# A float32 transpose on one core: PSUM evacuation split by halves, one copy for each evenly spaced run of ranges

## The chip, the cores and the metric

One core of one Trainium2 chip. The metric is the device time of one execution, in microseconds (us), as the median of several runs.

In the profiles PE is TensorE, PEld its weight loads, DVE is VectorE and ACT ScalarE; PEq and ACTq are the instruction streams of PE and of ScalarE, and L117 is a line of the kernel. PSUM is the memory into which PE transposes here, SBUF the one between it and the 16 DMA engines, which move the bytes in and out. A transfer has landed when its completion is signalled.

## The reference

```python
x = np.random.randn(8192, 8192).astype(np.float32)
def reference(x):
    return np.transpose(x)
```

268 MB are read and 268 MB written; nothing is computed.

## The kernel before

The input is cut into 128 chunks of 128 rows by 4096 columns, loaded whole into one of three buffers. PE transposes a chunk in 32 blocks of 128x128 into PSUM. Four blocks form a range `q` (512 columns of the input, 0 to 7), and a range is copied from PSUM to SBUF into a register: a buffer that gathers the same range of eight consecutive chunks, so that the store can write rows of 4 KB. The windows of the eight ranges are staggered, so in steady state one window closes, and is stored, in each chunk. There are nine registers for eight open windows: a window that opens in a chunk takes the register whose store was issued two chunks before.

```python
S = 32; B = 4; W = 8; NR = S // B; NIN = 3; NREG = 9
pss = [nc.alloc_psum_tensor(f"ps{k}", [P, 2 * B * P], dt).ap() for k in range(NR // 2)]
...
def transposes(k):                          # PE, one chunk
    nc.tensor.sem_inc(s_ld[k], -16).wait_op(s_ld[k], 16, "sem-ge")
    for h in range(NR // 2):
        if h < 2:                           # both copies of this engine in the last chunk are done
            n = NR // 4
            nc.tensor.sem_inc(s_bank[h], -n).wait_op(s_bank[h], n, "sem-ge")
        for b in range(2 * B):
            ...                             # transpose into pss[h]
        tr.then_inc(s_pe, 1)
...
for t, (s, c) in enumerate(chunks):
    for h in range(NR // 2):                # pairs of ranges (0,1) (2,3) (4,5) (6,7)
        e = h % 2
        eng = (nc.scalar, nc.vector)[e]     # ScalarE, VectorE, ScalarE, VectorE
        ...                                 # open windows; wait for the register's store
        eng.wait_ge(s_pe, t * NR // 2 + h + 1)
        for u in runs:                      # one run of two ranges, or two of one
            ...
            cp = nc.scalar.copy(out=o, in_=i) if e == 0 else nc.vector.tensor_copy(out=o, in_=i)
            ...
        for k in closing:
            store(*k)                       # issued by ScalarE, which first waits for that copy
    if t + NIN < T:
        nc.scalar.wait_ge(s_pe, (t + 1) * NR // 2)
        load(t + NIN)                       # issued by ScalarE too
```

ScalarE's stream therefore holds its copies, the waits for VectorE's copies whose windows close, and all stores and loads but the first three loads.

## Time and profile before

| | before |
|---|---|
| median of the first 3 runs | 1264.29 us (1264.04 to 1265.28) |
| PE busy | 742.7 us, 59% |
| VectorE busy | 316.1 us in 311 copies |
| ScalarE copies | 261.7 us in 320 copies |
| rate in mid-span, by fortieths of the span | 428 to 431 GB/s in most, 414 in the lowest |

Busy time is a share of the span, not of the critical path.

### The profile page before, as it was taken

The page shows a single profiled execution, that of the slowest core. Times are in us where ns is not written, and L with a number is a line of the kernel's source. Part 1 is how long each engine was busy: PE and PEld are TensorE (multiplying, and loading weights), DVE is VectorE, ACT ScalarE, POOL GpSimd, SP SyncE. Part 2 cuts the span into 40 slices and gives each one's busy share as a digit, 9 for nine tenths or more (in the row PEclk, how much of TensorE's full clock was granted, in tenths as well). Part 3 has the DMA queues.
Part 4 walks back from the last instruction along what each step waited for, and adds up shares of the span by engine and source line. Part 5 has one row for each costly group of instructions (what it writes and reads, how often), then busy time and mean ns, then how long its engine had stood idle before and what let it go on. Part 6 is the DMA issues. An engine that isn't in the chain of part 4 may idle for free. (4 is left out here: it accounts for less than half of the span.)

```text
span 1262.9 us, 9961 instructions
## 1 busy us (share of the span) xinstructions
PE 742.7 (59%) x4096; PEld 721.8 (57%) x4096; DVE 316.1 (25%) x311; ACT 263.0 (21%) x321; POOL 0.7 (0%) x6
## 2 busy tenths in 40 slices
PE   6565565665566555655566655666565655656561
PEld 5565555665566555655565655656565645655561
DVE  3322222222222222222222222222222222222220
ACT  3212121222122211212221121121212211122120
POOL 0000000000000000000000000000000000000000
PEclk9967768677777777686766687777868687777865
DMA  9999999999999999999999999999999999999998
GB/s 381 429 430 420 429 431 428 430 429 431 428 430 430 431 428 429 430 430 430 426 425 414 429 430 429 430 430 430 428 430 430 431 428 430 430 430 429 430 427 339
DMA packets 39274, 536.98 MB, mean 425 GB/s; under 512 B 4320, under 2 KB 4832, under 8 KB 6240
## 3 DMA queue, kind: packets, MB, share of 16 engines
q10 hardware_dynamic: 38832, 530.60, 98.8%
q1 hardware_dynamic: 432, 6.29, 1.2%
q14 instruction: 9, 0.07, 0.0%
q8 instruction: 1, 0.02, 0.0%
HBM read 268.44 MB, written 268.44 MB: 425 GB/s over the span
## 5 line engine op out<-in xcount | busy, mean ns | idle before, releaser
L117 PE MATMUL ps<-ident,in 128*128 128x128 f32 x4096 | 742.7, 364 | 493.1 <-PEq L114 493.1
L117 PEld LDWEIGHTS ps<-ident,in 128*128 128x128 f32 x4096 | 721.8, 219 | 513.9 <-issue 513.6
L208 DVE COPY regs<-ps 128x1024 f32<-128x1024 f32 (+1 forms) x311 | 316.1, 1034 | 921.2 <-PE ps L117 704.5
L208 ACT COPY regs<-ps 128x1024 f32<-128x1024 f32 (+1 forms) x320 | 261.7, 843 | 973.6 <-PE ps L117 654.9
L208 ACT ACT_TABLE_LOAD x1 | 1.3, 1283 | 0.9 <-SPq L69 0.9
L86 POOL TENSOR_SCALAR_AFFINE_SELECT ident<-ident 128x128 f32<-128x128 f32 x1 | 0.3, 293 | 0.2 <-POOL ident L84 0.2
L84 POOL MEMSET ident<- 128x128 f32 x1 | 0.2, 204 | 0.5 <-SPq L69 0.5
L241 POOL MEMSET const-bfloat16-1.0<- 128x1 bf16 x1 | 0.1, 102 | 0.0
L241 POOL MEMSET const-uint8-127<- 128x1 uint8 x1 | 0.1, 102 | 0.0
L241 POOL MEMSET const-float32-0.0<- 128x1 f32 x1 | 0.1, 99 | 0.2 <-issue 0.2
L241 POOL MEMSET const-float32-1.0<- 128x1 f32 x1 | 0.1, 99 | 0.0
## 6 DMA issues: line engine op xcount, KB each, us to landing
in<-in_x_dram ACTq DMA_DIRECT2D x125, 2048.0 KB, 22.5
out_dram<-regs ACTq DMA_DIRECT2D x114, 2048.0 KB, 18.4
out_dram<-regs ACTq DMA_DIRECT2D x4, 1792.0 KB, 17.5
in<-in_x_dram SPq DMA_DIRECT2D x3, 2048.0 KB, 11.6
out_dram<-regs ACTq DMA_DIRECT2D x4, 1536.0 KB, 15.1
out_dram<-regs ACTq DMA_DIRECT2D x4, 1280.0 KB, 16.7
out_dram<-regs ACTq DMA_DIRECT2D x4, 1024.0 KB, 16.6
out_dram<-regs ACTq DMA_DIRECT2D x4, 768.0 KB, 16.4
```

Of the source, the lines that this page charges most:

```text
L84: nc.gpsimd.memset(ident, 0.0).then_inc(s_id, 1)
L86: nc.gpsimd.affine_select(out=ident, in_=ident, compare_op=mybir.AluOpType.not_equal, fill=1.0, base=0, pattern=[[-1, P]], channel_multipl ...
L117: tr = nc.tensor.transpose(pss[h][:, b * P:(b + 1) * P], ins[k][:, j:j + B * P - B + 1:B], ident,)
L208: cp = nc.scalar.copy(out=o, in_=i) if e == 0 else nc.vector.tensor_copy(out=o, in_=i)
L241: nc = _bacc.Bacc("TRN2", target_bir_lowering=False, num_devices=1)
```

## The change

The intent: ScalarE takes ranges 0 to 3 and VectorE 4 to 7, each half in one PSUM tensor of four banks, so that up to four ranges whose places in the registers are evenly spaced go in one instruction. A half of PSUM is handed back to PE by one signal, after its last copy. A copy waits for the last range that it reads.

```diff
-        pss = [nc.alloc_psum_tensor(f"ps{k}", [P, 2 * B * P], dt).ap() for k in range(NR // 2)]
+        NH = NR // 2
+        pss = [nc.alloc_psum_tensor(f"ps{k}", [P, NH * B * P], dt).ap() for k in range(2)]
...
-            for h in range(NR // 2):
-                if h < 2:
-                    n = NR // 4
-                    nc.tensor.sem_inc(s_bank[h], -n).wait_op(s_bank[h], n, "sem-ge")
+            for q in range(NR):
+                e, g = divmod(q, NH)
+                if g == 0:
+                    nc.tensor.sem_inc(s_bank[e], -1).wait_op(s_bank[e], 1, "sem-ge")
...
-            for h in range(NR // 2):
-                e = h % 2
+            for e in range(2):
...
-                for q in (2 * h, 2 * h + 1):
+                for q in range(e * NH, (e + 1) * NH):
...
+                runs = []
+                for g in range(NH):
+                    if runs:
+                        ...          # same window length and the same gap as the run so far
+                            u.append(g)
+                            continue
+                    runs.append([g])
...
+                    eng.wait_ge(s_pe, t * NH + (e * NH + u[-1]) // 2 + 1)
...
-                for k in closing:
-                    store(*k)
+                    for q in ends:
+                        store(q, e, copied[e])
```

## The prediction

> **What bounds the kernel now.** I read the page's slices and its queue lines first, because a transpose computes nothing and must move every byte twice.
>
> ```profile
> DMA  9999999999999999999999999999999999999998
> GB/s 381 429 430 420 429 431 428 430 429 431 428 430 430 431 428 429 430 430 430 426 425 414 429 430 429 430 430 430 428 430 430 431 428 430 430 430 429 430 427 339
> ...
> q10 hardware_dynamic: 38832, 530.60, 98.8%
> q1 hardware_dynamic: 432, 6.29, 1.2%
> ...
> HBM read 268.44 MB, written 268.44 MB: 425 GB/s over the span
> ```
>
> The mean busy share of the 16 DMA engines is at least nine tenths in 39 of the 40 slices, and the two data queues' packets fill 98.8 + 1.2 = 100% of the 16 engines' time. The rate is flat at 428 to 431 GB/s between a ramp and a tail. No compute engine comes near: PE 59%, VectorE 25%, ScalarE 21% of 1262.9 us. The table of stretches says the same without the ends:
>
> ```profile
> 100.00:600.00 500.00, 298.56 (x1632) 290.33 (x1632) 125.62 (x120) 103.64 (x118) 0.00 (x0) 0.75 1.01 429
> 600.00:1100.00 500.00, 301.13 (x1632) 292.90 (x1632) 125.75 (x122) 104.03 (x123) 0.00 (x0) 0.74 1.01 428
> ```
>
> The last three columns are the granted clock, the DMA share and GB/s: share 1.01, so there is no hole between transfers to win back. At 429 GB/s a chunk's 2.097 MB in and 2.097 MB out take 4.89 us each, 9.78 us a chunk; 128 chunks make 1252 us, and what remains of the 1262.9 us span is the start (first transposes at 8.46 us) and the drain of the last stores.
>
> A bound DMA can still be starved if copies make issues late, so I then looked at one chunk's timeline (start us, length us, engine, what) and at how far ahead of need the transfers are issued:
>
> ```profile
> 444.96 6.14 PEld L117 LDWEIGHTS ps<-ident,in 128*128 128x128 f32 x32 [3.82 <-issue]
> 445.00 6.30 PE L117 MATMUL ps<-ident,in 128*128 128x128 f32 x32 [3.65 <-PEq L114]
> 446.99 1.01 ACT L208 COPY regs<-ps 128x1024 f32<-128x1024 f32 x1 [5.51 <-PE ps L117]
> 448.69 1.23 DVE L208 COPY regs<-ps 128x1024 f32<-128x1024 f32 x1 [6.09 <-PE ps L117]
> 450.39 1.01 ACT L208 COPY regs<-ps 128x1024 f32<-128x1024 f32 x1 [2.39 <-PE ps L117]
> 451.40 1.23 DVE L208 COPY regs<-ps 128x1024 f32<-128x1024 f32 x1 [1.48 <-PE ps L117]
> 452.66 0.55 ACTq L28 DMA_DIRECT2D out_dram<-regs  x1
> 453.24 1.23 ACTq L100 DMA_DIRECT2D in<-in_x_dram  x1
> ```
>
> ```profile
> in<-in_x_dram ACTq DMA_DIRECT2D x125, 2048.0 KB, 22.5
> out_dram<-regs ACTq DMA_DIRECT2D x114, 2048.0 KB, 18.4
> ```
>
> PE works 6.3 us of each 9.8 us and idles 3.65 us for the next load; each copy waits for PE. A load lands 22.5 us and a store 18.4 us after issue, though its own transfer takes 4.89 us. The very first load was issued at 0.94 us and its transposes began at 8.46 us: 7.5 us, so about 2.6 us of fixed latency above the 4.89. What is left is time spent behind other transfers: 22.5 - 4.9 - 2.6 = 15.0 us for a load, 18.4 - 4.9 - 2.6 = 10.9 us for a store. That is the slack: issues may come that much later before the DMA engines run dry.
>
> **What the Trainium skill says.** "DMA: Bandwidth & Descriptors", section Where 436 GB/s comes from, puts the ceiling of the 16 SBUF ports at 435.2 GB/s. The trace agrees: it sits at 428 to 431, 1 to 2% below. (The same section says that about 358 GB/s binds for HBM to SBUF; it also says that its single-core numbers are of one core with its neighbour idle, as one core runs here, and the trace shows 430.) "ScalarE: Activation LUTs", section What ACT_TABLE_LOAD costs, gives 186 ns + 0.833 ns per element for an ACTIVATE with immediate scale and bias, and an overlap of about 93 ns between back-to-back ones. The trace's two ScalarE forms, below, give 165 + 0.828 per element, and two adjacent 128x512 copies show 1.07 us together, not 2 x 589 ns. "VectorE: DVE Perf Modes", section Why PSUM operands drop a tier, says that an fp32 operand in PSUM holds VectorE at one element a cycle; the trace's 1.05 ns per element agrees with the page's 0.96 GHz. So VectorE is not sped up by a longer instruction.
>
> **The change part by part.** The rows by form:
>
> ```profile
> L208 DVE COPY regs<-ps 128x1024 f32<-128x1024 f32 x201 | 245.3, 1224 | 707.4 <-PE ps L117 542.0 <-DMA out_dram<-regs 163.9
> L208 ACT COPY regs<-ps 128x1024 f32<-128x1024 f32 x192 | 193.5, 1013 | 740.3 <-PE ps L117 486.9 <-DMA out_dram<-regs 209.9 <-DVE regs L208 39.9
> L208 DVE COPY regs<-ps 128x512 f32<-128x512 f32 x110 | 70.9, 686 | 213.8 <-PE ps L117 162.5 <-DMA out_dram<-regs 50.9
> L208 ACT COPY regs<-ps 128x512 f32<-128x512 f32 x128 | 68.7, 589 | 233.3 <-PE ps L117 168.0 <-DMA out_dram<-regs 50.4 <-DVE regs L208 7.2
> ```
>
> Each engine still copies 4 of 8 ranges of 512 elements per chunk, the same amount. What the built kernels' instruction streams show: ScalarE goes from 320 copies to 256 (40 of four ranges, 32 of three, 72 of two, 112 of one: 160 + 96 + 144 + 112 = 512 ranges), VectorE from 311 to 250 (45, 25, 77, 103). A longer copy, by the rows' slopes: ScalarE 424 ns per further range, so 589 + 3 x 424 = 1861 ns for four; VectorE 538 ns, so 686 + 3 x 538 = 2300 ns. Because neighbours overlap, a merged copy saves only 1.07 - 1.01 = 0.06 us on ScalarE and 1.29 - 1.23 = 0.06 us on VectorE (pairs of 128x512 in the timeline against one 128x1024). So ScalarE loses about 64 x 0.06 = 4 us of 262, VectorE 61 x 0.06 = 4 us of 316, all beside other work. The PE's transposes, and sizes, number and order of the transfers stay.
>
> What moves is when a range is copied. PE finishes a range every 6.3 / 8 = 0.79 us. Store issue after the start of PE's pass, before and after, no register wait, worst case of one copy of four:
> - ranges 0, 1: before one copy behind range 1, 2.0 + 1.0 + 0.1 = 3.1 us. After: behind range 3, 3.2 + 0.3 + 1.9 = 5.4. Later by 2.3.
> - ranges 2, 3: VectorE's first copy ended at 449.92, 5.0 us. After 5.4. Later by 0.4.
> - ranges 4, 5: ScalarE's second copy ended at 451.40, 6.4 us. After, on VectorE behind range 7: 6.3 + 0.2 + 2.3 = 8.8. Later by 2.4.
> - ranges 6, 7: 7.7 us (452.66 - 444.96). After 8.8. Later by 1.1.
>
> The load follows in ScalarE's stream: at worst at 8.8 + 0.6 = 9.4 us where it was 6.5 to 8.3, later by 3 us. All of this is set against slacks of 10.9 us (store) and 15.0 us (load), and the lateness does not add up from chunk to chunk as long as loads land every 9.8 us: the queue gets the same transfers in the same order, later by a constant. Sum on the path that sets the end: 0.
>
> PSUM: PE may start a half when that half's copies are done, ScalarE's at 5.4 us (6.6 if it first waits for a register, which the timeline shows freed 4.7 us after PE's start: 4.7 + 1.9), VectorE's at 8.8. The next pass begins at 9.8 and reaches the second half at 9.8 + 3.2. Neither waits.
>
> The ends. In the first chunks PE was held 0.29 to 0.46 us between passes by the last ScalarE copy; in the change that copy comes earlier, since ScalarE's ranges are PE's first four. The ramp loses about 1 us to a low rate (14 to 30 us: 400 GB/s in the mean against 430, 7% of 16 us), so at most some tenths can come back. At the end the eight closing stores have the same sizes and order and the same bytes to drain (2048 + 1792 + ... + 256 KB = 9.4 MB, 22 us at 430 GB/s). Sum: -0.3 us, so 1264.3 becomes 1264.0.
>
> **The rivals.**
> - *The stores' feedback becomes the bound.* There are 9 registers for 8 open windows, so a window opened at a chunk needs the store issued two chunks before; the waits view has 260 us of ScalarE and 215 us of VectorE waiting on stores, and now such a wait holds all four ranges of an engine. If the delays above were exposed, 0.2 us per chunk (25 / 128) would already be 2%, and 2 us per chunk would make 1500 us. Against it: the awaited store lands 4.7 us into PE's pass, before PE has finished the ranges, and the 10.9 us of slack is four times the delay.
> - *PE waits for PSUM.* Four banks are now released by one signal each, after one long copy. If PE slipped past the load it would show as a longer gap before its passes. It has 3.65 us of idle time per chunk, and VectorE's release at 8.8 us precedes the need at 13 us. Even if 1 us were exposed in each chunk, loads are 15 us ahead: 1264 still.
> - *It gets faster because ScalarE, which issues all but the first three transfers, is freer.* 4 us of 262 us is freed, but nothing moves faster. 536.98 MB at the skill's 435.2 GB/s is 1234 us without any ramp or drain; 2% faster is 1239, which leaves 5 us for a start and a tail that in steps of 2 us show 41 and 270 GB/s before full rate, and 208, 74 and 8 after it. Practically excluded.
>
> **Range and chances.** Three runs of before lie within 1.2 us. I add 2 us for a changed ramp or tail and for the phase of reads and writes against each other, either way: 1260.5 to 1267.5. Faster by over 2%: 0.01. Slower by over 2%, if the slack is not what I read out of the landing times: 0.02. Within: 0.97.
>
> **What would show it.** Right: the DMA row again nines with 428 to 431 GB/s and queue shares adding to 100%; ScalarE near 258 us in 256 copies, VectorE near 312 in 250; four-range copies near 1.86 and 2.30 us; store and load landing times shorter by 1 to 3 us, the eaten slack. Wrong: eights or less in the DMA row, mid-span rates under 425, landing times near 8 us (the queue run dry), or PE waiting for a bank rather than for its load.

## The result and the profile after

| | before | after |
|---|---|---|
| median of 6 runs | 1264.2 us (1264.04 to 1265.28) | 1263.88 us (1263.51 to 1265.03) |
| ratio after / before | | 0.9997, 95% interval 0.9984 to 1.001 |
| ScalarE copies | 320, 261.7 us | 256, 251.5 us |
| VectorE copies | 311, 316.1 us | 250, 302.7 us |
| load, store: median issue to landing | 22.5, 18.4 us | 21.7, 17.5 us |

A ratio is the mean time of one kernel's runs over that of the other's of the same rounds, so it is not quite the ratio of the medians. Executions over 1.5% slower than the fastest of the same kernel are left out of the means. The two kernels are the same within the noise.

The two rows of the page of the kernel after, in 40 slices of its span: busy tenths of the DMA engines, and their rate.

```profile
DMA  9999999999999999999999999999999999999998
GB/s 381 429 429 428 430 430 428 430 429 431 428 430 430 429 428 431 429 429 430 429 423 413 431 428 431 428 430 429 431 428 430 429 430 430 429 430 429 430 419 346
```

The rate is where it was. The dip to 413 has its like before (414). One chunk's timeline in the kernel after (start us, length us, engine, what; the lines of PEld are left out):

```profile
434.79 6.22 PE L118 MATMUL ps<-ident,in 128*128 128x128 f32 x32 [3.75 <-PEq L116]
438.49 1.87 ACT L216 COPY regs<-ps 128x2048 f32<-128x2048 f32 x1 [7.90 <-PE ps L118]
440.17 2.36 DVE L216 COPY regs<-ps 128x1024 f32<-128x1024 f32 x2 [7.63 <-PE ps L118]
442.56 0.55 ACTq L28 DMA_DIRECT2D out_dram<-regs  x1
443.14 1.21 ACTq L102 DMA_DIRECT2D in<-in_x_dram  x1
444.55 6.43 PE L118 MATMUL ps<-ident,in 128*128 128x128 f32 x32 [3.53 <-PEq L116]
```

Four alternating copies have become one ScalarE copy of four ranges, which starts once range 3 is there, and in this chunk two VectorE copies of two ranges, back to back. The last copy ends at 442.53, 2.0 us before PE's next pass, and PE still idles 3.5 us ahead of that pass, so nothing of the longer copies reaches it here. The store is issued 7.8 us into the pass. The durations of the longest copies, from the groups of the kernel after by shape:

```profile
L216 DVE COPY regs<-ps 128x2048 f32<-128x2048 f32 x45 | 103.1, 2292 | 332.1 <-PE ps L118 332.1
L216 ACT COPY regs<-ps 128x2048 f32<-128x2048 f32 x40 | 74.7, 1866 | 310.5 <-PE ps L118 247.5 <-DMA out_dram<-regs 63.0
```

2292 and 1866 ns were predicted as 2300 and 1861.

### The profile page after: what moved, and what is told of

It is laid out like the page before. It is cut to its first block, busy times and chain, and to the rows that moved or that the text cites. A ratio compares the mean times of both kernels' runs of the same rounds, so it can differ in the third digit from the quotient of the medians.

```text
span 1262.4 us, 9794 instructions
## 1 busy us (share of the span) xinstructions
PE 749.6 (59%) x4096; PEld 729.1 (58%) x4096; DVE 302.7 (24%) x250; ACT 252.8 (20%) x257; POOL 0.7 (0%) x6
## 5 line engine op out<-in xcount | busy, mean ns | idle before, releaser
L118 PEld LDWEIGHTS ps<-ident,in 128*128 128x128 f32 x4096 | 729.1, 220 | 506.5 <-issue 506.5
L216 DVE COPY regs<-ps 128x512 f32<-128x512 f32 (+3 forms) x250 | 302.7, 1246 | 934.4 <-PE ps L118 823.4
L216 ACT COPY regs<-ps 128x512 f32<-128x512 f32 (+3 forms) x256 | 251.5, 1015 | 981.9 <-PE ps L118 491.1
## 6 DMA issues: line engine op xcount, KB each, us to landing
in<-in_x_dram ACTq DMA_DIRECT2D x125, 2048.0 KB, 21.7
out_dram<-regs ACTq DMA_DIRECT2D x114, 2048.0 KB, 17.5
```

Of the source, the lines that this page charges most:

```text
L118: tr = nc.tensor.transpose(pss[e][:, (g * B + b) * P:(g * B + b + 1) * P], ins[k][:, q * B * P + b:(q + 1) * B * P - B + b + 1:B], ident,)
```

## The experiments

Twelve kernels ran. The time is the median of the fast runs.

| label | time, us | against the kernel before |
|---|---|---|
| single_ranges | 1264.68 | 0.9999 (0.9982 to 1.0016) |
| copies_x2 | 1271.02 | 1.0047 (1.0027 to 1.0067) |
| copies_x3 | 1327.37 | 1.0495 (1.0478 to 1.0513) |
| copies_x4 | 1633.08 | 1.2904 (1.2877 to 1.293) |
| loads_late | 1346.77 | 1.0643 (1.0615 to 1.0671) |
| before_light, wrong | 629.42 | 0.498 (0.4972 to 0.4989) |
| after_light, wrong | 604.91 | 0.4786 (0.4778 to 0.4794) |
| before_light_held, wrong | 608.59 | 0.4805 (0.4794 to 0.4816) |
| after_light_single, wrong | 561.92 | 0.4437 (0.4427 to 0.4447) |
| before_8regs | 1352.47 | 1.0696 (1.0661 to 1.0731) |
| after_8regs | 1317.96 (fast runs; 1318.21 of all five) | 1.0421 (1.0403 to 1.0438) |
| before_8regs_held | 1353.63 | 1.0695 (1.066 to 1.073) |

### Undoing the merging alone

single_ranges keeps the new split but never joins ranges.

```diff
-                    if runs:
+                    if False:
```

> The changed kernel with its new split of the ranges but one instruction for each range (512 copies an engine), so the merging alone is undone. Theory: 1264 us, within 0.2%; ScalarE near 265 us busy, VectorE near 320. Rival (the number of instructions on the engine that issues the transfers matters): 1 to 2% slower than 1264 us.

Measured: 1264.68 us, 0.9999; ScalarE 272.4 us and VectorE 318.3 us in 512 copies each. In the full kernel the number of copies costs nothing that the noise lets us see. It also measures what a merge saves. Against these, the changed kernel has 256 ScalarE copies fewer in 20.9 us less, 0.08 us each, and 262 VectorE copies fewer in 15.6 us less, 0.06 us each.

### Making the copies longer

Each copy is done n times, n = 2, 3, 4, and each repeat waits until the one before has ended.

```diff
+                    for _ in range(n - 1):
+                        cp = nc.scalar.copy(out=o, in_=i) if e == 0 else nc.vector.tensor_copy(out=o, in_=i)
+                        cp.then_inc(s_x[e], 1)
+                        extra[e] += 1
+                        eng.wait_ge(s_x[e], extra[e])
                     cp = nc.scalar.copy(out=o, in_=i) if e == 0 else nc.vector.tensor_copy(out=o, in_=i)
```

> The changed kernel with every copy out of PSUM done twice, the second after the first has ended (same data, right result). Theory (the DMA engines bound it and the copies lie in the slack of 10 us that is left before a store is due): 1264 us, within 0.3%, with VectorE near 620 us busy, ScalarE near 510, and the stores' median time to landing about 2 us shorter than the 17.5 us of the changed kernel. Rival (the stores' feedback through the registers exposes a later copy): 2 to 3 us more in each of 128 chunks, 1500 to 1650 us.

> Every copy done three times. VectorE then needs about 3 x 2.36 us and some waits, 8 us of each 9.8 us chunk in most chunks and near 9.9 us where it has four single ranges. Theory: 1264 to 1285 us, the excess only where single ranges saturate VectorE; stores land about 5 us sooner after issue than 17.5 us. Rival (feedback): over 1700 us.

> Every copy done four times, as a control that the copies can bind at all. VectorE needs 4 x 2.36 us and waits of about 1.4 us, some 11 us of a chunk. Theory: VectorE becomes the bound, 1380 to 1480 us, VectorE busy share over 80%, DMA row below 9. Rival: if even this stays at 1264 us, the copies overlap in a way that I do not see.

Measured: 1271, 1327 and 1633 us. Doubling the work of both copy engines (VectorE 614 us busy, ScalarE 510) costs 0.5%, so most of a copy lies beside the transfers; the rival's 2 to 3 us per chunk is refuted. But 0.5% is more than the 0.3% that the theory allowed, though the interval, 0.27 to 0.67%, still reaches it. The rate was 405 GB/s in the first 100 us (413 in the kernel before) and 425 from 600 to 1100 us (428). The stores land 15.4 us after issue (17.5 in the changed kernel), so on the reckoning of the prediction there should have been eight more microseconds of room. x3 was expected to end by 1285 us, and its start is only part of the excess: its first 135 us ran at 327 GB/s (416 before) with a DMA share of 0.83, which is 135 x 89 / 416 = 29 us of the 63 us, and the stretch from 600 to 1100 us ran at 410 GB/s. Over the whole run its stores land 13.0 us after issue, in the median. x4 was expected at 1480 us at most, on VectorE as the bound; VectorE is busy 76% of the profiled 1638 us, not the expected 80% and more, so waits take part too; I take them to be in the ring of copies, stores and loads, which no run here isolates. The expected time was too low in all three, in the first by little.

### Issuing the loads one chunk later

This takes lead from the loads without making any copy longer.

```diff
+            if t and t - 1 + NIN < T:
+                load(t - 1 + NIN)
             if t + NIN < T:
                 nc.scalar.wait_ge(s_pe, (t + 1) * NR // 2)
-                load(t + NIN)
```

> The changed kernel with each load issued one chunk later, just behind that chunk's store, so that a load has one chunk (9.8 us) less of lead. Theory of the prediction (a load may come 15.0 us later before the DMA engines run dry): about 1264 us, up to 1%, with loads landing near 12 us after issue. Rival (the rate falls already when less is queued, as the twice done copies hint, 0.5% for 2 us): 2 to 8% slower, the DMA share still at nine tenths or more.

Measured: 1346.8 us, 6.4% slower: the rival. From loads_late, the stretch 100 to 600 us (the last three columns are the granted clock, the DMA share and GB/s), and the transfers' landing times:

```profile
100.00:600.00 500.00, 284.14 (x1546) 276.39 (x1545) 112.83 (x80) 94.42 (x80) 0.00 (x0) 0.74 0.99 404
...
in<-in_x_dram ACTq DMA_DIRECT2D x125, 2048.0 KB, 13.9
out_dram<-regs ACTq DMA_DIRECT2D x114, 2048.0 KB, 9.5
```

The loads still land 13.9 us after issue, 6.4 us above the 7.5 us that the very first one needed, so by the prediction's reckoning the engines never run dry. And the share of busy time agrees with that: 0.99. Yet the rate has fallen from 429 to 404 GB/s. Two readings of the prediction fail at once. The busy share did not tell a saturated DMA from one that loses 6%; only the rate did. And the lead that a landing time shows is not all slack. Ordered by how long a store takes to land, the profiles read:

| kernel | store lands after, us | rate over the span, GB/s |
|---|---|---|
| before | 18.4 | 425 |
| single_ranges | 17.9 | 425 |
| after | 17.5 | 425 |
| copies_x2 | 15.4 | 423 |
| copies_x3 | 13.0 | 405 |
| loads_late | 9.5 | 400 |
| before_8regs_held | 8.7 | 398 |
| before_8regs | 8.6 | 397 |
| copies_x4 | 7.7 | 328 |

The rate over the span is the time in another unit (537 MB over the span), and these kernels differ in more than the queue (x3 also has its slow start), so this is an ordering, not a law; loads_late alone changes nothing but when the loads are issued. after_8regs is left out, since its profile is of a slow run.

The packet records of the kept traces show where the rate goes. From 100 to 1100 us, the median packet of 16 KB took 611 ns in the kernel after and in loads_late alike, and 16 engines that move 16,384 bytes in 611 ns make 429 GB/s: the mid-span rate is engines at work on packets back to back. What grew is a tail: 0.3% of these packets took over 700 ns in the kernel after, 8.1% in loads_late (mean 979 ns). That tail makes up the whole rise of the mean, from 614 to 643 ns. Slow packets count as busy time, so the share stays at 0.99. What makes these packets slow, a short queue or a changed mix of loads and stores, was not settled.

### Taking the transfers' bound away

Both kernels with light transfers: after the first three loads each load brings a sixteenth of the columns, and each store but the first writes one of its four rows. The number of transfers, waits, passes and copies stays. Their outputs are wrong, which doesn't matter for the times.

```diff
+            cut = J if t < NIN else J // 16
...
-                out=ins[t % NIN], in_=x[c * P:(c + 1) * P, s * J:(s + 1) * J]
+                out=ins[t % NIN][:, :cut], in_=x[c * P:(c + 1) * P, s * J:s * J + cut]
...
+                if any(stored):
+                    dst, src = dst[:, :1], src[:, :rows]
```

> The changed kernel with the DMA bound taken away (wrong result on purpose): after the first three, each load brings a sixteenth of the columns, and each store but the first writes one of its four rows; the PE passes, copies, waits and number of transfers are unchanged. Theory: PE's passes bind, 4.1 to 6.6 us each by the granted clock, 600 to 870 us, and the two light kernels lie within 3% of each other, because both splits free their banks before PE comes back to them. Rival (the longer copies hold PE at the half that it needs next): the light kernel after is over 3% slower than the light kernel before, 0.3 us or more in each of 128 chunks.

> The kernel before with the same cut loads and stores (wrong result on purpose). Theory: 600 to 870 us, within 3% of the light kernel after; PE may be held 0.3 us a pass by the last ScalarE copy, as in the first chunks of the trace, so if either is faster it is the kernel after.

Measured: 629.42 us before, 604.91 after, 24.5 us or 3.9% less (604.91 / 629.42 = 0.961). The direction was expected, the size was not: both theories had the two kernels within 3%, or the kernel after behind. PE is now busy 86 and 87% of the span, at a granted clock of 0.99 where the full kernels had 0.74, so its passes are shorter too (4.1 us). So there is a gain in the change under these conditions, and the full kernel does not show it. Two more kernels ask which part it comes from.

In the light kernel before, ScalarE's stream has a store between its two copies in the chunks in which a window of VectorE's first pair of ranges closes. From its timeline (120 to 175 us; PEld left out):

```profile
137.86 4.08 PE L118 MATMUL ps<-ident,in 128*128 128x128 f32 x32 [0.52 <-PEq L115]
139.09 1.01 ACT L211 COPY regs<-ps 128x1024 f32<-128x1024 f32 x1 [1.38 <-PE ps L118]
140.12 1.22 DVE L211 COPY regs<-ps 128x1024 f32<-128x1024 f32 x1 [1.52 <-PE ps L118]
141.38 0.48 ACTq L28 DMA_DIRECT2D out_dram<-regs  x1
141.90 1.01 ACT L211 COPY regs<-ps 128x1024 f32<-128x1024 f32 x1 [1.79 <-DVE regs L211]
...
143.06 4.11 PE L118 MATMUL ps<-ident,in 128*128 128x128 f32 x32 [1.12 <-PEq L115]
```

VectorE's copy ends at 141.34; only then is the store issued, and only behind it does ScalarE's second copy start. It ends at 142.91, and PE, whose pass ended at 141.94, starts its next one at 143.06. before_light_held issues the stores at the end of the chunk:

```diff
+            held = []
             for h in range(NR // 2):
...
-                for k in closing:
-                    store(*k)
+                held += closing
+            for k in held:
+                store(*k)
             if t + NIN < T:
```

> The light kernel before (629.4 us against 604.9 for the light kernel after), with one thing of the change alone: its stores are issued at the end of the chunk, after both of ScalarE's copies. In the light kernel before, the store of ranges 2 and 3 lies between ScalarE's two copies and waits there for VectorE (46.8 us over 25 waits; none in the light kernel after), while PE waits for the bank that the second copy frees. Theory (this order in ScalarE's stream is what the light kernel before loses): 603 to 612 us. Rival (the bank or split of ranges, or the number of copies, makes the difference): 624 to 632 us.

after_light_single undoes the merging in the light kernel after, with the same one-line edit as single_ranges:

> The light kernel after with one copy for each range, so the merging alone is undone. Theory (order of ScalarE's stream): 603 to 609 us as with merged copies. Rival (fewer copies are the gain): 615 us or more.

Measured: 608.59 us for the held stores, as the theory said. In the chunk shown above PE now starts 0.23 us after its last pass in place of 1.12 (120 to 150 us of its timeline):

```profile
139.10 4.33 PE L118 MATMUL ps<-ident,in 128*128 128x128 f32 x32 [0.23 <-PEq L115]
```

So the order in ScalarE's stream alone is worth 20.8 us in the kernel before. That is not yet a share of the 24.5 us of the change, because the other kernel fell outside both expectations: 561.92 us, 43 us (7.1%) faster than with merged copies. (These two ran in another call than the first two, on a chip where the kernel before took 1265.12 us against 1264.28.) The new split with its order of stores is worth 67.5 us, more than the whole change, and merging takes 43 us of it back; how much of the 67.5 us is the order of stores was not measured in that split. The waits of PE for its sequencer in the light kernel after with merged copies, then with single ones:

```profile
PE ps L119 <- PEq L117: 65.6, 92, 8.6
```

```profile
PE ps L119 <- PEq L117: 34.5, 34, 8.7
```

92 stops have become 34. (PE's waits fell by 31.1 us; its busy time, which the profile models, fell from 525.8 to 516.3 us.) The timeline of the light kernel after shows how a merged copy makes one (PEld left out):

```profile
360.71 2.29 DVE L219 COPY regs<-ps 128x2048 f32<-128x2048 f32 x1 [2.36 <-PE ps L119]
363.04 0.48 ACTq L28 DMA_DIRECT2D out_dram<-regs  x1
363.21 2.17 PE L119 MATMUL ps<-ident,in 128*128 128x128 f32 x16 [0.60 <-PEq L117]
363.56 0.60 ACTq L103 DMA_DIRECT2D in<-in_x_dram  x1
364.20 1.93 ACT L219 COPY regs<-ps 128x512 f32<-128x512 f32 x2 [4.76 <-issue]
...
366.27 7.99 PE L119 MATMUL ps<-ident,in 128*128 128x128 f32 x64 [0.89 <-PEq L117]
```

VectorE's copy of four ranges starts only when range 7 is there and ends at 363.00. PE's second half waits for it, the store waits for it, and ScalarE, held by that store and the load behind it, starts its own copies at 364.20, after an idle time of 4.76 us. They end at 366.13 and PE goes on at 366.27. A copy for each range runs beside PE instead. That is a reading of one stretch; that the merging is the cause is shown by the pair of kernels.

### Exposing the stores' feedback

```diff
-    NREG = 9
+    NREG = 8
```

> The changed kernel with 8 registers in place of 9, so that a window waits for the store of the chunk just before. Theory: now the feedback is exposed, and both kernels are slower; a store issued 8 us into a pass and landing 8 to 12 us later at the least gives a period of 11 to 16 us, 1400 to 2000 us. The change issues stores up to 2.4 us later and holds all four ranges, so I expect the kernel after to be 2 to 15% slower than the kernel before here. Rival (no feedback through registers): both stay at 1264 us.

> The kernel before with 8 registers. Theory: 1400 to 1900 us, faster than the kernel after with 8 registers. Rival: 1264 us.

Measured: 1318 us after (its four fast runs; a fifth run of 1336 us was slow, and the profile fell on it), 1352 us before. Both are slower, so the feedback is there, but far less than expected, and the kernel after is 2.6% the faster one (1.0421 / 1.0696 = 0.974), where I expected it to be slower by 2 to 15%. I then took the stream's order, which explained the light pair, as the cause, and put the held stores into the kernel before with 8 registers:

> The kernel before with 8 registers (1352 us) and its stores issued at the end of each chunk, after both of ScalarE's copies. Theory: the change was the faster one with 8 registers (1318 us) because ScalarE was not held, between its two copies, by a store that waits for a VectorE that waits for a register (123.2 us over 16 waits); then this gives 1310 to 1330 us. Rival (the split itself, or the time at which stores of ranges 0 and 1 go out): 1345 us or more, these stores now being later.

Measured: 1353.6 us, no change. This theory fell. Something in the split itself, or in the merging, is worth 2.6% with 8 registers; which one, these runs don't say.

## Why the prediction was right

The time was 1263.88 us; 1264.0 and "same" were predicted. The verdict follows from the mechanism; the match in tenths is luck (see The ends). By its steps:

- **What binds.** The mid-span rate is the same in both kernels (429 GB/s from 100 to 600 us, 428 from 600 to 1100), and no fortieth of a span in any profile here is above 432 GB/s. Copies removed (single_ranges against after) move nothing, and bytes removed take over half of the time away. Right. The rate was not as flat as the prediction read it: its own row has 420, 425 and 414 in mid-span, so single slices of both kernels meet its sign "mid-span rates under 425", which therefore says nothing. One support was weaker than I made it: a busy share of 1.01 was read as "no hole", and loads_late has 0.99 at 404 GB/s.
- **Counts and durations.** 256 and 250 copies, 1866 and 2292 ns: right. The saved busy time was mis-sized: 4 us an engine predicted, 10.2 us (ScalarE) and 13.4 us (VectorE) measured. The term was 0.06 us per merge, taken from pairs inside one evacuation. It left out that an engine's two evacuations per chunk stood apart before and stand together now: VectorE's two 128x1024 copies took 2 x 1.23 us before and take 2.36 us back to back, and 2.29 us as one copy of four ranges.
- **Issue times.** Predicted for a VectorE half at the worst 8.8 us after the start of PE's pass; in a chunk with a copy of four, the pass began at 161.51 us and the copy ended at 170.15 us, 8.6. Landing times shrank by 0.8 and 0.9 us, under the predicted 1 to 3, presumably because the worst case is not every chunk's.
- **The slack.** Enough for this change, but its size was wrong. 10.9 us for a store and 15.0 us for a load were to be the time until the engines run dry, with nothing lost before; copies_x2 loses 0.5% with 3 us of the store's lead gone, loads_late 6.4% with one chunk's lead. The change used 0.9 us.
- **PSUM.** PE's idle time before a pass stayed 3.5 us in the full kernel. Right there. In the light kernel the merged copies do hold PE, against the expectation of after_light; the prediction's reckoning was for a pass every 9.8 us.
- **The ends.** The first three passes now run without a gap, as predicted (96 transposes in 14.10 us), but the fourth starts at 25.32 us where it started at 25.28, since it waits for its load. The 0.3 us predicted for this was not earned there, and the 0.3 us measured is within the noise.
- **The rivals.** None set the time. The first was partly there: ScalarE's waits for stores grew from 260.3 to 478.8 us (VectorE's shrank from 214.8 to 111.0), since a wait now holds all four ranges of an engine, but they lie beside the transfers; with 8 registers they cost 4.2 and 7.0%. Against the third, ScalarE freed for issuing, stands single_ranges: 20.9 us more of ScalarE's copies, the same time. The 1234 us there is an estimate from the ceiling on the skill's page.

Where the expected gain went: the copies were not on the path that sets the time. What the change is worth with light transfers, 3.9% at the higher clock, does not show as long as 537 MB pass at 429 GB/s.

## What to carry to other kernels

When a kernel moves bytes at a flat rate through its whole span, as this one, expect nothing from a change to the engines beside it until the bytes get fewer; look at the rate, not at the busy share, and at how early transfers are issued. Treat the lead seen in landing times as an upper bound on slack, and test it with a variant that issues later. Where copies do bind, a longer copy saves its start-up but starts when its last input is there and frees its buffer when its last element is out; and a store that waits for another engine should not lie between two copies of the engine that issues it (worth 20.8 us in the light kernel, nothing with 8 registers).

## What the Trainium skill lacked or had wrong

- "DMA: Bandwidth & Descriptors", Where 436 GB/s comes from, says that for transfers between HBM and SBUF about 358 GB/s binds. Here one core held 428 to 431 GB/s with reads and writes in equal parts, near the 435 that the section gives for the fabric and the 425 that it quotes from a measurement. The 358 is half of what two cores share, by the same section; no run here had both cores streaming.
- "Perfetto Trace Analysis", Identifying the Most-Contended Engine, calls DMA occupancy misleading with 16 engines. The runs agree and put a size on it: shares of 1.01 and 0.99 in mid-span go with 429 and 404 GB/s.
- No page gives how the rate depends on how far ahead transfers are issued. With each load of 2 MB issued one chunk later and nothing else changed, it fell here from 429 to 404 GB/s from 100 to 600 us, at a DMA share of 0.99, through the 8% of slow packets.
- "Perfetto Trace Analysis", Optimizing Scalar/DVE Operations, says both that grouping operations can help where the engine is saturated and that breaking them up can help where it causes bubbles elsewhere, but gives no size. The light kernels, with VectorE busy 50%, are the second case: 604.9 us grouped, 561.9 us broken up.
- "ScalarE: Activation LUTs", What ACT_TABLE_LOAD costs: 186 ns + 0.833 ns per element would be 1892 ns for 2048 elements, an estimate from the page; copies of 128x2048 from PSUM took 1866 ns, 1.4% less.
